# First-layer expert weights in pieces of 512 rows by 512 columns, and wide experts that sum four blocks side by side

## The chip, the cores and the metric

The kernel runs on one core of one Trainium2 chip. The metric is the device time of one execution in microseconds (us). The engines are named as in the profile: PE (TensorE, matmuls), PEld (its weight loads), DVE (VectorE), ACT (ScalarE), POOL (GpSimd) and SP (SyncE, which here only issues DMAs).

## The reference, cut to what matters

One layer of a model with 1024 tokens of width 1024: layer norm, a mixer (attention and a recurrence), layer norm, and then a mixture of 32 experts, of which each token uses 4. The change is in the experts alone.

```python
def clamped_swiglu(hh):
    x_glu = jnp.minimum(hh[..., ::2], SWIGLU_LIMIT)
    x_lin = jnp.clip(hh[..., 1::2], -SWIGLU_LIMIT, SWIGLU_LIMIT)
    return x_glu * jax.nn.sigmoid(SWIGLU_ALPHA * x_glu) * (x_lin + 1.0)
...
    def expert_block(args):
        idx, e = args
        u = clamped_swiglu(h_pad[idx] @ w1[e] + b1[e])
        return u @ w2[e] + b2[e]
```

For one expert `w1` has 1024 rows (the model width) and 2048 columns (a gate column and a linear column for each of 1024 hidden units), and `w2` has 1024 rows and 1024 columns. All of it is float32.

## The kernel before

The mixer and the routing take about the first 1000 us. The routing ranks the experts by their number of tokens, and the kernel gives each rank a fixed capacity: the eleven fullest ranks have room for 136 to 192 tokens (wide experts), the other 21 for 128 (thin experts). A loop for what overflows makes no pass with these inputs. The method `moe` goes through the 32 experts in a fixed order: the first and third are thin, the second and fourth wide, and from then on two thin experts alternate with one wide one, with one thin expert at the end.

Each expert reads 12 pieces of weights of 1 MB, 8 of `w1` and 4 of `w2`, through the method `piece`. A piece arrives by one DMA in a buffer `w` (5 of them). To keep float32 accuracy the kernel multiplies in two parts: ACT makes a rounded copy `wsh` (line 205, two halves of 128 x 1024), and DVE subtracts it to give the rest, `wsl` (line 206, also two halves). There are 4 buffers for such a pair, so at most 4 pieces are split ahead of the matmuls. A `w` buffer is free again when DVE is done with it; a `wsh`/`wsl` buffer is free when the last matmul on that piece is done.

A thin expert (method `first`) keeps its tokens as the stationary operand and streams the weights. Each of four accumulators `acc` (one PSUM bank, 128 x 512) takes two pieces of 256 columns by all 1024 rows: for each piece 8 row blocks, three matmuls each (tokens high by weights high, high by low, low by high; lines 193, 194, 195). ACT and DVE then compute the activation, PE transposes it, and ACT and DVE split the transposes (`uTh`, `uTl`) for the second layer, which streams 512 columns at a time.

A wide expert (method `first_wide`) turns the operands round: 128 weight columns are stationary, and the tokens are streamed, high and low parts side by side (line 1511, up to 384 columns) against `wsh`, and the high part again (line 1513) against `wsl`. Before the change a piece gives two accumulators one after the other (gate and linear part of one block of 128 hidden units), each of 16 matmuls over all 1024 rows. ACT reads an accumulator (line 1515), then DVE (line 1516); only then is its buffer free. There are four accumulator buffers, used in turn by both layers of all experts.

The kernel is written without fixed places in time: the framework's scheduler sets, when the program is built, in which order the instructions stand on each engine, and each engine then works strictly through its list. A DMA is issued on SP's queue when its `w` buffer is free.

Of the kernel before, what the change touches and what calls it, by code (L numbers as in the profile page):

```python
# [10 lines left out]
F32 = mybir.dt.float32  # L11
# [8 lines left out]
P = 128  # L20
# [3 lines left out]
KD = D // P  # L24
# [3 lines left out]
NE = 32  # L28
# [46 lines left out]
def _cols(v):  # L75
    return np.asarray(v).reshape(-1, P).T
# [25 lines left out]
def prep(a):  # L102

    f = lambda n: np.asarray(a[n])
    o = {}
    inv = (np.float32(10000.0) ** (-np.arange(0, 32, 2, dtype=np.float32) / np.float32(32))).astype(np.float32)
    invf = np.tile(np.repeat(inv, 2), 4).reshape(P, 1)
    sgn = np.tile(np.array([-1.0, 1.0], np.float32), 64).reshape(P, 1)
    o["vec"] = np.concatenate(
        [_cols(f("c")), _cols(f("emb_ln_g")), _cols(f("emb_ln_b")), _cols(f("ada_b")[0, :2048]),  # L110
         _cols(f("q_norm_g")), _cols(f("kv_norm_g")), _cols(f("mla_out_g")), _cols(f("rwkv_mu")),
         _cols(f("rwkv_k_k")), _cols(f("rwkv_k_a")), _cols(f("rwkv_r_k")), _cols(f("rwkv_gn_g")),
         _cols(f("rwkv_gn_b")), _cols(f("rwkv_a0")), _cols(f("ln1_g")), _cols(f("ln1_b")), invf, sgn], axis=1)
    o["cst"] = consts()
    o["thr"] = (np.array(CAP)[None, :] + P * np.arange(NB)[:, None]).astype(np.float32)[None]
    o["x"] = f("x")[0]
    o["pos"] = f("positions")
    aw = f("ada_w")[0]
    o["ada1"] = aw[:, :2048].reshape(KD, P, 4, 512).transpose(2, 1, 0, 3)
    o["ada2"] = aw[:, 2048:].reshape(KD, P, 8, 512).transpose(2, 1, 0, 3)  # L120
    o["adab2"] = f("ada_b")[:, 2048:]
    o["rows"] = np.stack([f(n).reshape(-1) for n in ROWS])
    w = f("w_in")[0]
    swap = np.arange(32) ^ 1
    blocks = [w[:, 0:128], w[:, 128:256], w[:, 256:384],
              np.concatenate([w[:, 384:416], w[:, 384:416][:, swap], np.zeros((D, 64), w.dtype)], axis=1)]
    blocks += [w[:, 416 + 128 * i:416 + 128 * (i + 1)] for i in range(14)]
    o["w_in"] = np.stack([b.reshape(KD, P, P).transpose(1, 0, 2) for b in blocks])
    q = f("w_uq")[0].reshape(256, NH, 96)
    rope = q[:, :, 64:].reshape(256, 256)  # L130
    rsw = q[:, :, 64:][:, :, swap].reshape(256, 256)
    q = np.concatenate([q[:, :, :64].reshape(256, 512), rope, rsw], axis=1)
    o["w_uq"] = q.reshape(2, P, 1024).transpose(1, 0, 2)
    o["w_uk"] = f("w_uk")[0]
    o["w_uv"] = f("w_uv")[0]
    o["w2a"] = np.concatenate([f("rwkv_w2")[0], f("rwkv_w0")], axis=0)
    o["a2"] = f("rwkv_a2")[0]
    o["g2"] = f("rwkv_g2")[0]
    o["w_o"] = f("w_o")[0].reshape(KD, P, D).transpose(1, 0, 2)
    o["rw"] = f("router_w")[0].reshape(KD, P, NE).transpose(1, 0, 2)  # L140
    o["rb"] = f("router_b")

    w1 = f("exp_w1")[0].reshape(NE, KD, P, 8, P, 2)
    o["w1"] = w1.transpose(0, 3, 2, 1, 5, 4).reshape(NE, 8, P, KD, 256)
    o["w2"] = f("exp_w2")[0].reshape(NE, 4, 2, P, D).transpose(0, 1, 3, 2, 4)
    b1 = f("exp_b1")[0].reshape(NE, 8, P, 2).transpose(0, 1, 3, 2)

    o["b1r"] = np.concatenate([b1.reshape(NE, 4, 512)] * 2, axis=1)
    o["b2"] = f("exp_b2")[0]
    o["b1c"] = b1.reshape(NE, 16, P).transpose(0, 2, 1)  # L150
    return {k: np.ascontiguousarray(v) for k, v in o.items()}
# [12 lines left out]
class Build:  # L164
# [705 lines left out]
    def head(self, h, oT):  # L870
# [64 lines left out]
        yield  # L935

    def mixers(self, st, left, first, oT, dst):


# [508 lines left out]
    def first(self, e, xT):  # L1448

        nc, mp, pm = self.nc, self.mo, self.pm  # L1450
        V, S, G = nc.vector, nc.scalar, nc.gpsimd
        w1 = self.i["w1"]
        bs = self.biases(e)
        u = mp.tile([P, D], F32, name="u")
        uT = self.split_tile(mp, [P, KD, P], "uT")
        for q in range(4):
            acc = pm.tile([P, 512], F32, name="acc", bufs=4)
            nc.tensor.matmul(acc, self.pick[:, q:q + 1].to_broadcast([P, P]), bs, start=True, stop=False)
            for j in range(2):
                ws = self.piece(w1[bass.ds(e, 1), 2 * q + j].rearrange("o p k n -> (o p) (k n)"))  # L1460
                for k in range(KD):
                    w, c = ws[k // 4], k % 4 * 256
                    self.mm(acc[:, j * 256:(j + 1) * 256], xT[:, k], w[:, c:c + 256],
                            start=False, stop=(j == 1 and k == KD - 1))
            a = acc.rearrange("p (j g f) -> p j g f", j=2, g=2)
            v2 = lambda t: t.rearrange("p (j f) -> p j f", j=2)
            sg = mp.tile([P, 256], F32, name="sg")
            S.activation(v2(sg), a[:, :, 0], AF.Sigmoid, scale=1.702)  # L1468
            ln = mp.tile([P, 256], F32, name="ln")
            V.tensor_scalar(v2(ln), a[:, :, 1], 8.0, -6.0, ALU.min, ALU.max)  # L1470
            V.scalar_tensor_tensor(v2(ln), a[:, :, 0], 7.0, v2(ln), ALU.min, ALU.mult)
            V.scalar_tensor_tensor(u[:, q * 256:(q + 1) * 256], sg, SIG7, ln, ALU.min, ALU.mult)
            if q:
                self.flip(uT, u, 2 * q - 2, 2 * q)
        return [uT], lambda: self.flip(uT, u, 6, 8)
# [14 lines left out]
    def first_wide(self, e, xw, slots):  # L1490

        nc, mp, pm = self.nc, self.mo, self.pm
        V, S, G = nc.vector, nc.scalar, nc.gpsimd
        cap = xw.shape[3]
# [5 lines left out]
        u1 = self.u1  # L1500
        n1 = cap - P
        w1 = self.i["w1"]
        for j in range(KD):
            ws = self.piece(w1[bass.ds(e, 1), j].rearrange("o p k n -> (o p) (k n)"))
            parts = []
            for g in range(2):
                acc = pm.tile([P, 512], F32, name="acc", bufs=4)
                for k in range(KD):
                    w = ws[k // 4]
                    c = slice(k % 4 * 256 + g * P, k % 4 * 256 + (g + 1) * P)  # L1510
                    nc.tensor.matmul(acc[:, 0:2 * cap], w.hi[:, c], xw[:, k].rearrange("p a t -> p (a t)"),  # L1511
                                     start=(k == 0), stop=False)
                    nc.tensor.matmul(acc[:, 0:cap], w.lo[:, c], xw[:, k, 0], start=False, stop=(k == KD - 1))  # L1513
                t = mp.tile([P, cap], F32, name=f"t{g}")
                S.activation(t, acc[:, cap:2 * cap], AF.Identity, bias=bc[:, 2 * j + g:2 * j + g + 1])
                V.tensor_tensor(t, acc[:, 0:cap], t, ALU.add)  # L1516
                parts.append(t)
# [270 lines left out]
```

## Time and profile before

| | |
|---|---|
| median of 3 runs | 2482.98 us (2480.03 to 2487.98) |
| the profiled execution | 2487.42 us |
| its span, first to last instruction | 2485.6 us |
| mean granted PE clock over the span | 0.953 of full speed |
| expert loop, about 995 to 2420 us | PE busy 1385.55 of 1425.00 us, DVE 1286.28 |

The profiled execution is 4.4 us above the median of the runs shown, and 1.8 us of its time lie outside the span. Busy time of PE is a modelled union of overlapping matmuls, so the pace of matmuls is better read from their start times than from their durations.

### The profile page before, as it was taken

How to read it: one execution, taken by the hardware profiler on the slowest of the kernel's cores; microseconds unless marked ns; L12 is line 12 of the kernel's file. 1: busy time of each engine (PE TensorE's matmuls, PEld its weight loads, DVE VectorE, ACT ScalarE, POOL GpSimd, SP SyncE). 2: the span in 40 equal slices, each digit the busy share in tenths (PEclk: the TensorE clock that was granted, in tenths of full speed). 3: DMA queues.
4: the chain of work that ended last, by engine and by line, in shares of the span. 5: the costliest groups of instructions: out<-in, count | busy, mean ns of one | idle time of the engine just before them, and what ended most of it. 6: DMA issues, size and time to landing. Idle time of an engine off the chain costs nothing. (4 is left out here: it accounts for less than half of the span.)

```text
span 2485.6 us, 41948 instructions
## 1 busy us (share of the span) xinstructions
PE 2314.4 (93%) x15523; PEld 1957.1 (79%) x15523; DVE 1994.8 (80%) x3854; ACT 1411.2 (57%) x2357; POOL 558.7 (22%) x411
## 2 busy tenths in 40 slices
PE   6999999999999897799999999999999999999992
PEld 3776766776766685699899898999989988889981
DVE  7666446677766676789898989898979999898987
ACT  5323334444545433566676666676757766666664
POOL 1005222222222444022121212121402121121113
PEclk9999988999989987799999999999999999999996
DMA  6377542212112223779797979797978989797973
GB/s 266 118 258 275 188 112 55 53 45 59 36 40 58 97 96 117 297 279 332 290 339 277 350 275 358 269 359 270 363 265 319 331 307 322 288 334 284 341 279 139
DMA packets 167334, 567.80 MB, mean 228 GB/s; under 512 B 64616, under 2 KB 79737, under 8 KB 116820
## 3 DMA queue, kind: packets, MB, share of 16 engines
q1 hardware_dynamic: 155476, 524.63, 57.4%
q0 software_dynamic: 11216, 39.34, 6.4%
q8 instruction: 124, 2.03, 0.3%
q10 hardware_dynamic: 432, 1.09, 0.1%
q14 instruction: 86, 0.70, 0.1%
HBM read 508.22 MB, written 56.79 MB: 227 GB/s over the span
## 5 line engine op out<-in xcount | busy, mean ns | idle before, releaser
L206 DVE TENSOR_TENSOR wsl<-w,wsh 128x1024 fp32r<-128x1024 f32 x786 | 935.3, 1221 | 139.3 <-ACT wsh L205 138.0
L205 ACT CAST wsh<-w 128x1024 fp32r<-128x1024 f32 x786 | 782.9, 1047 | 348.9 <-PE acc L195 91.0
L193 PE MATMUL acc<-wsh,xTh 128*128 128x256 f32 x1344 | 381.9, 285 | 9.5 <-ACT xTh L205 5.1
L1511 PE MATMUL acc<-xw,wsh 128*128 128x368 f32 (+7 forms) x1408 | 379.0, 352 | 6.4 <-DVE t L1516 6.3
L194 PE MATMUL acc<-wsl,xTh 128*128 128x256 f32 x1344 | 382.8, 285 | 0.7 <-DVE wsl L206 0.7
L195 PE MATMUL acc<-wsh,xTl 128*128 128x256 f32 x1344 | 381.6, 285 | 0.1
L1513 PE MATMUL acc<-xw,wsl 128*128 128x184 f32 (+7 forms) x1408 | 337.2, 240 | 0.0
L1511 PEld LDWEIGHTS acc<-xw,wsh 128*128 128x128 f32 x1408 | 268.0, 190 | 8.5 <-issue 5.2
L1513 PEld LDWEIGHTS acc<-xw,wsl 128*128 128x128 f32 x1408 | 272.2, 193 | 1.0 <-DVE wsl L206 0.2
L193 PEld LDWEIGHTS acc<-wsh,xTh 128*128 128x128 f32 x1344 | 258.5, 193 | 12.6 <-ACT xTh L205 7.0
L194 PEld LDWEIGHTS acc<-wsl,xTh 128*128 128x128 f32 x1344 | 259.5, 193 | 4.8 <-DVE wsl L206 1.0
L195 PEld LDWEIGHTS acc<-wsh,xTl 128*128 128x128 f32 x1344 | 259.2, 193 | 1.5 <-DVE xTl L206 0.3
L1445 POOL DMA_INDIRECT y_d<-y,idx x42 | 147.4, 3509 | 417.9 <-DVE y L1437 327.6
L1348 POOL DMA_INDIRECT xg<-h_d,idx x43 | 92.1, 2142 | 612.9 <-issue 285.0
L193 PE MATMUL acc<-wsh,uTh 128*128 128x512 f32 x512 | 204.5, 402 | 20.3 <-ACT uTh L205 20.3
L194 PE MATMUL acc<-wsl,uTh 128*128 128x512 f32 x512 | 203.2, 397 | 0.0
L195 PE MATMUL acc<-wsh,uTl 128*128 128x512 f32 x512 | 193.5, 405 | 1.8 <-DVE uTl L206 1.8
L193 PEld LDWEIGHTS acc<-wsh,uTh 128*128 128x128 f32 x512 | 97.6, 191 | 42.0 <-ACT uTh L205 23.1
L193 PE MATMUL sm<-hTh,wsh 128*128 128x512 f32 x288 | 116.6, 405 | 7.5 <-ACT wsh L205 2.0
L194 PE MATMUL sm<-hTl,wsh 128*128 128x512 f32 x288 | 117.0, 406 | 4.2 <-DVE hTl L347 3.1
L195 PE MATMUL sm<-hTh,wsl 128*128 128x512 f32 x288 | 115.1, 400 | 0.0
L194 PEld LDWEIGHTS acc<-wsl,uTh 128*128 128x128 f32 x512 | 98.0, 191 | 19.2
(582 smaller groups left out, 4382.0 us busy)
## 6 DMA issues: line engine op xcount, KB each, us to landing
w<-in_w_dram SPq DMA_DIRECT2D x384, 1024.0 KB
aw<-in_ada_dram SPq DMA_DIRECT2D x34, 512.0 KB
w<-in_w_in_dram SPq DMA_DIRECT2D x18, 512.0 KB
aw<-in_ada_dram SPq DMA_DIRECT2D x7, 1024.0 KB
rkv_d<-stage SPq DMA_DIRECT2D x12, 512.0 KB
xt<-in_x_dram SPq DMA_DIRECT2D x8, 512.0 KB
xr<-in_x_dram SPq DMA_DIRECT2D x8, 512.0 KB
xr_d<-xr SPq DMA_DIRECT2D x8, 512.0 KB
```

The lines of the kernel that those rows point to most:

```text
L193: mm(out, a.hi, b.hi, start=start, stop=False)
L194: mm(out, a.hi, b.lo, start=False, stop=False)
L195: mm(out, a.lo, b.hi, start=False, stop=stop)
L205: (hi_eng or self.nc.scalar.copy)(dst.hi, src)
L206: (lo_eng or self.nc.vector).tensor_tensor(dst.lo, src, dst.hi.bitcast(F32), ALU.subtract)
L1348: self.nc.gpsimd.indirect_dma_start(out=xg[0:n], out_offset=None, in_=self.h2_d, in_offset=bass.IndirectOffsetOnAxis(ap=idx[0:n, 0:1], axi ...
L1445: nc.gpsimd.indirect_dma_start(out=self.y_d, out_offset=bass.IndirectOffsetOnAxis(ap=idx[0:n, 0:1], axis=0), in_=y[0:n], in_offset=None, c ...
L1511: nc.tensor.matmul(acc[:, 0:2 * cap], w.hi[:, c], xw[:, k].rearrange("p a t -> p (a t)"), start=(k == 0), stop=False)
L1513: nc.tensor.matmul(acc[:, 0:cap], w.lo[:, c], xw[:, k, 0], start=False, stop=(k == KD - 1))
```

## The change

Pieces of `w1` have another shape: 512 rows by 512 columns in place of 1024 rows by 256 columns. Their size (1 MB, 8 KB for each partition) and number stay, as do the splitting and all of the second layer. In a thin expert an accumulator still takes two pieces, now one for each half of the rows, and each matmul streams 512 columns in place of 256. In a wide expert two pieces hold four blocks of 128 columns; the kernel takes four accumulators at once, runs all four over the first piece, then over the second, and evaluates them as two pairs. Number and shapes of a wide expert's matmuls stay.

```diff
-    w1 = f("exp_w1")[0].reshape(NE, KD, P, 8, P, 2)
-    o["w1"] = w1.transpose(0, 3, 2, 1, 5, 4).reshape(NE, 8, P, KD, 256)
+    w1 = f("exp_w1")[0].reshape(NE, 2, 4, P, 4, 2, P, 2)
+    o["w1"] = w1.transpose(0, 4, 1, 3, 2, 5, 7, 6).reshape(NE, 8, P, 4, 512)
...
-            for j in range(2):
-                ws = self.piece(w1[bass.ds(e, 1), 2 * q + j].rearrange("o p k n -> (o p) (k n)"))
-                for k in range(KD):
-                    w, c = ws[k // 4], k % 4 * 256
-                    self.mm(acc[:, j * 256:(j + 1) * 256], xT[:, k], w[:, c:c + 256],
-                            start=False, stop=(j == 1 and k == KD - 1))
+            for m in range(2):
+                ws = self.piece(w1[bass.ds(e, 1), 2 * q + m].rearrange("o p k n -> (o p) (k n)"))
+                for k in range(4):
+                    c = k % 2 * 512
+                    self.mm(acc, xT[:, 4 * m + k], ws[k // 2][:, c:c + 512], start=False, stop=(m == 1 and k == 3))
...
+        accs = []
         for j in range(KD):
-            ws = self.piece(w1[bass.ds(e, 1), j].rearrange("o p k n -> (o p) (k n)"))
+            if j % 2 == 0:
+
+                accs = [pm.tile([P, 512], F32, name="acc", bufs=4) for _ in range(4)]
+                for m in range(2):
+                    ws = self.piece(w1[bass.ds(e, 1), j + m].rearrange("o p k n -> (o p) (k n)"))
+                    for a, acc in enumerate(accs):
+                        for k in range(4):
+                            w, c = ws[k // 2], slice(k % 2 * 512 + a * P, k % 2 * 512 + (a + 1) * P)
+                            x = xw[:, 4 * m + k]
+                            nc.tensor.matmul(acc[:, 0:2 * cap], w.hi[:, c], x.rearrange("p a t -> p (a t)"),
+                                             start=(m == 0 and k == 0), stop=False)
+                            nc.tensor.matmul(acc[:, 0:cap], w.lo[:, c], x[:, 0], start=False, stop=(m == 1 and k == 3))
             parts = []
             for g in range(2):
-                acc = pm.tile([P, 512], F32, name="acc", bufs=4)
-                for k in range(KD):
-                    w = ws[k // 4]
-                    c = slice(k % 4 * 256 + g * P, k % 4 * 256 + (g + 1) * P)
-                    nc.tensor.matmul(acc[:, 0:2 * cap], w.hi[:, c], xw[:, k].rearrange("p a t -> p (a t)"),
-                                     start=(k == 0), stop=False)
-                    nc.tensor.matmul(acc[:, 0:cap], w.lo[:, c], xw[:, k, 0], start=False, stop=(k == KD - 1))
+                acc = accs[j % 2 * 2 + g]
```

Three places show how the order of instructions changes. In the built program names carry numbers: `acc_13871` is one use of an accumulator buffer, `wsh_13875` one piece; the lines of the wide matmuls move from 1511 and 1513 to 1513 and 1515, and DVE's first read of an accumulator from 1516 to 1521.

On PE, in a thin expert, before: the last two of eight row blocks on one piece, and the first on the next.

```order
L193 MATMUL acc_13871<-wsh_13875,xTh_13719 128x256
L194 MATMUL acc_13871<-wsl_13876,xTh_13719 128x256
L195 MATMUL acc_13871<-wsh_13875,xTl_13720 128x256
L193 MATMUL acc_13871<-wsh_13907,xTh_13719 128x256
L194 MATMUL acc_13871<-wsl_13908,xTh_13719 128x256
L195 MATMUL acc_13871<-wsh_13907,xTl_13720 128x256
```

The same place now: the last of four row blocks on one piece, and the first on the next.

```order
L193 MATMUL acc_13295<-wsh_13299,xTh_13143 128x512
L194 MATMUL acc_13295<-wsl_13300,xTh_13143 128x512
L195 MATMUL acc_13295<-wsh_13299,xTl_13144 128x512
L193 MATMUL acc_13295<-wsh_13319,xTh_13143 128x512
L194 MATMUL acc_13295<-wsl_13320,xTh_13143 128x512
L195 MATMUL acc_13295<-wsh_13319,xTl_13144 128x512
```

A piece had 24 matmuls of 256 columns and has 12 of 512; pieces follow each other in the same way.

On PE, in the fourth wide expert (176 tokens), before: where one accumulator follows another; each has its 16 matmuls in a row, of which the first or last pair stands here.

```order
L1511 MATMUL acc_14443<-xw_14174,wsh_14437 128x352
L1513 MATMUL acc_14443<-xw_14174,wsl_14438 128x176
...
L1511 MATMUL acc_14463<-xw_14174,wsh_14437 128x352
L1513 MATMUL acc_14463<-xw_14174,wsl_14438 128x176
```

The same expert now, from the last matmul of its second group of four to the first of its fourth: 8 matmuls for each accumulator and piece, of which the first stands here.

```order
L1515 MATMUL acc_13766<-xw_13502,wsl_13810 128x176
L1513 MATMUL acc_13877<-xw_13502,wsh_13883 128x352
...
L1513 MATMUL acc_13878<-xw_13502,wsh_13883 128x352
...
L1513 MATMUL acc_13879<-xw_13502,wsh_13883 128x352
...
L1513 MATMUL acc_13877<-xw_13502,wsh_13923 128x352
...
L1513 MATMUL acc_13880<-xw_13502,wsh_13883 128x352
...
L1513 MATMUL acc_13880<-xw_13502,wsh_13923 128x352
...
L1513 MATMUL acc_13991<-xw_13502,wsh_13997 128x352
```

Three accumulators now run over both pieces, and the fourth, `acc_13880`, comes last; it uses the buffer of `acc_13766`, and both pieces stay in use until it is done.

On DVE, in the same expert, before: one piece is split (two halves), then an accumulator is read.

```order
L206 TENSOR_TENSOR wsl_14609<-w_14606,wsh_14608 128x1024 x2
L1516 TENSOR_TENSOR t1_14423<-acc_14406,t1_14423 128x176
L206 TENSOR_TENSOR uTl_14320<-t1_14366,uTh_14319 128x128
L206 TENSOR_TENSOR u1_8922<-t1_14366,u1_8922 128x48
L1516 TENSOR_TENSOR t0_14460<-acc_14443,t0_14460 128x176
```

The same engine now: two pieces are split one after the other, then `acc_13766` is read.

```order
L1521 TENSOR_TENSOR t0_13862<-acc_13765,t0_13862 128x176
L206 TENSOR_TENSOR xTl_14106<-tr_14114,xTh_14105 128x512
L206 TENSOR_TENSOR uTl_13648<-t1_13751,uTh_13647 128x128
L206 TENSOR_TENSOR u1_8922<-t1_13751,u1_8922 128x48
L206 TENSOR_TENSOR wsl_13998<-w_13995,wsh_13997 128x1024 x2
L206 TENSOR_TENSOR wsl_14038<-w_14035,wsh_14037 128x1024 x2
L1521 TENSOR_TENSOR t1_13865<-acc_13766,t1_13865 128x176
L1521 TENSOR_TENSOR t0_13961<-acc_13877,t0_13961 128x176
```

The read that frees the fourth accumulator's buffer now stands behind four halves of weights where it stood behind two.

## Rows read from the trace of the kernel before

**Rows 1.** The page, parts 1 and 2: busy time by engine; granted clock in 40 slices.
```profile
span 2485.6 us, 41948 instructions
PE 2314.4 (93%) x15523; PEld 1957.1 (79%) x15523; DVE 1994.8 (80%) x3854; ACT 1411.2 (57%) x2357; POOL 558.7 (22%) x411
...
PEclk9999988999989987799999999999999999999996
```

**Rows 2.** Busy time by stretch, the whole expert loop.
```profile
core 0: us, PE busy (x) PEld busy (x) DVE busy (x) ACT busy (x) POOL busy (x), PEclk, DMA share, GB/s
995.00:2420.00 1425.00, 1385.55 (x9617) 1273.54 (x9615) 1286.28 (x2070) 961.28 (x1475) 268.99 (x99) 0.98 0.85 310
```

**Rows 3.** The same view: a wide stretch, then a stretch of two thin experts.
```profile
1417.00:1475.00 58.00, 58.00 (x378) 53.25 (x378) 49.53 (x98) 36.87 (x70) 6.49 (x4) 1.00 0.76 270
1475.00:1549.00 74.00, 72.91 (x538) 67.38 (x538) 73.29 (x98) 53.69 (x70) 20.36 (x5) 1.00 0.95 350
```

**Rows 4.** The page, part 5: matmul groups, count, busy, mean ns, idle before.
```profile
L193 PE MATMUL acc<-wsh,xTh 128*128 128x256 f32 x1344 | 381.9, 285 | 9.5 <-ACT xTh L205 5.1
...
L1511 PE MATMUL acc<-xw,wsh 128*128 128x368 f32 (+7 forms) x1408 | 379.0, 352 | 6.4 <-DVE t L1516 6.3
...
L1513 PE MATMUL acc<-xw,wsl 128*128 128x184 f32 (+7 forms) x1408 | 337.2, 240 | 0.0
```

**Rows 5.** PE in order of time, thin experts: start, duration; brackets: idle before.
```profile
1533.21 0.28 PE L193 MATMUL acc<-wsh,xTh 128*128 128x256 f32 x1
...
1536.81 0.28 PE L193 MATMUL acc<-wsh,xTh 128*128 128x256 f32 x1
...
1538.56 0.39 PE L193 MATMUL acc<-wsh,uTh 128*128 128x512 f32 x1
...
1539.92 0.38 PE L1360 MATMUL tr<-csts,u 128*128 128x128 f32 x2
1540.77 0.50 PE L193 MATMUL acc<-wsh,uTh 128*128 128x512 f32 x1 [0.46 <-ACT uTh L205]
```

**Rows 6.** PE in order of time, second layer of the thin expert before.
```profile
1505.79 0.40 PE L193 MATMUL acc<-wsh,uTh 128*128 128x512 f32 x1
...
1507.40 0.39 PE L194 MATMUL acc<-wsl,uTh 128*128 128x512 f32 x1
```

**Rows 7.** Who waited for whom, 1060 to 2400 us: total, times, longest.
```profile
ACT wsh L205 <- PE acc L195: 89.3, 95, 3.3
...
PE acc L193 <- ACT uTh L205: 12.2, 10, 2.6
...
PE acc L1511 <- DVE t L1516: 6.3, 6, 2.0
```

**Rows 8.** PE in a wide expert: last matmul of one accumulator, and of the next.
```profile
1430.98 0.24 PE L1513 MATMUL acc<-xw,wsl 128*128 128x176 f32 x1
...
1433.17 0.24 PE L1513 MATMUL acc<-xw,wsl 128*128 128x176 f32 x1
```

**Rows 9.** ACT in the same stretch.
```profile
1433.37 2.00 ACT L205 CAST wsh<-w 128x1024 fp32r<-128x1024 f32 x2 [1.16 <-PE acc L1511]
1435.27 0.40 ACT L1515 ACTIVATE t<-acc,bc 128x176 f32<-128x176 f32 x1
```

**Rows 10.** DVE in the same stretch.
```profile
1434.45 2.36 DVE L206 TENSOR_TENSOR wsl<-w,wsh 128x1024 fp32r<-128x1024 f32 x2 [0.23 <-ACT wsh L205]
1436.72 0.34 DVE L1516 TENSOR_TENSOR t<-acc,t 128x176 f32<-128x176 f32 x1
```

**Rows 11.** PE at one wait for an accumulator.
```profile
1840.04 0.59 PE L1511 MATMUL acc<-xw,wsh 128*128 128x304 f32 x1 [2.01 <-DVE t L1516]
```

**Rows 12.** Busy time and granted clock around that wait.
```profile
1836.00:1848.00 12.00, 9.99 (x56) 9.85 (x55) 8.87 (x25) 7.75 (x18) 0.00 (x0) 0.72 0.68 250
```

**Rows 13.** PE in the first expert, waiting for its fourth piece.
```profile
1025.66 0.58 PE L193 MATMUL acc<-wsh,xTh 128*128 128x256 f32 x1 [4.38 <-ACT wsh L205]
```

## Prediction, made before the changed kernel ran

> **What bounds the kernel now.** I first read the page for where the time lies. PE is busy 93% of the span and its granted clock is at nine tenths or more in all but the last of the later slices [rows 1], which are the expert loop, where the change is. Then I read busy time by stretch. Over the loop PE is busy 1385.55 of 1425.00 us, DVE 1286.28 [rows 2], so PE sets the pace on average, with about 40 us idle. Next I took one wide and one two-thin stretch apart, since an average over both hides their limits. In the wide stretch PE is busy all 58.00 us and DVE only 49.53; in the thin one PE is busy 72.91 of 74.00 us and DVE 73.29 [rows 3]. So thin experts are limited by two engines at once, and DVE has room only in wide ones. Waits say the same from the other side: ACT waited 89.3 us for PE to free a split-weight buffer in thin first layers, while PE itself waited 12.2 us for `uTh` and 6.3 us for a wide accumulator [rows 7]. The splitters run ahead; PE seldom waits for them. Last I read the pace of matmuls from start times.
>
> **Thin first layers: fewer, longer matmuls.** The 256-column matmuls start every 0.120 us: 30 of them from 1533.21 to 1536.81 [rows 5]. The 512-column matmuls of the second layer have the same float32 type and the same stationary tile size, and start every 0.227 us: 6 from 1538.56 to 1539.92 [rows 5]. A longer look one expert earlier gives 7 in 1.61 us, or 0.230 [rows 6]. Two short ones cost 0.240 us, so one long one saves 0.010 to 0.013 us. Line 193 has 1344 short matmuls [rows 4], lines 194 and 195 as many: 4032 become 2016 of double length. That gives 2016 x 0.010 = 20 us to 2016 x 0.013 = 26 us; I take the middle, 24 us, or 1.15 us for each of 21 thin experts. The weight loads halve with the matmuls and lie beside them, so they are not counted again.
>
> The same rows can be set against a rule. The Trainium skill (TensorE: Matmul & The Clock Gate, section Back-to-back issue gap) gives a warm gap of the columns divided by 2.4 GHz plus about 2.5 ns, that is 109 ns and 216 ns here. By that rule an exchanged pair saves 2.6 ns and all 2016 together some 5 us, an estimate from that page. The trace does not agree with it: its 120 and 227 ns carry 13 to 14 ns of extra for each matmul.
>
> **What stays.** DMAs, ACT casts and DVE splits keep their number and size, and the three streaming matmuls of a row block keep their order; a thin accumulator is complete after the same two pieces. I cost these at nothing: the piece DMAs are hidden by five buffers, and without that cover each late piece would be a wait like the one in the first expert. There PE waited 4.38 us for its fourth piece [rows 13], since the loop has only just begun to load. A faster first layer only waits longer there, so that expert's 1.15 us are not gained: +1 us.
>
> **Wide first layers: the same matmuls, another order.** The 2 x 1408 matmuls of lines 1511 and 1513 [rows 4] keep their shapes, so their own price is zero. What moves is when buffers come free. A pair of matmuls takes 0.274 us (8 pairs from 1430.98 to 1433.17) [rows 8]. Before, a buffer is wanted again after three more accumulators, 3 x 2.19 = 6.6 us. Its readers are done sooner: after the last matmul at 1433.17 ACT first casts a piece (2.00 us), reads at 1435.27 [rows 9], DVE splits that piece (2.36 us) and reads at 1436.72 to 1437.06 [rows 10], 3.9 us in all, so 2.7 us are left over.
>
> After the change I follow `acc_13766`, at the end of a group of four, with the same durations. PE goes on with three accumulators on both pieces: 24 pairs, 6.6 us, and a few transposes or slot matmuls; then `acc_13880` wants its buffer. ACT has two pieces to cast first, and the first of them goes into a buffer that came free 8 matmuls (1.1 us) before the end. So the casts end about 1.1 us less than 2 x 2.00, at +3.0 us, and at +4.1 if ACT is busy when that buffer comes free. DVE can finish the second piece 1.2 us behind the last cast and then read: 4.5 to 5.6 us, and one more us if the small operations listed ahead of the splits are late. The buffer is free 0 to 2 us before it is wanted. Three such hand-overs in each of 11 wide experts make 33. Most fit, some will miss by a few tenths: I take 0.15 us each, +5 us. The bounds are -6 us (the 6.3 us of today's waits vanish [rows 7]) and one more split piece, 2.36 us less 1 us of slack, at each of the 33: +45 us.
>
> **Thin stretches: what DVE gives back.** Two thin experts shrink by 2.3 us on PE, but DVE has 73.29 us of work in a stretch of 74.00 [rows 3], so only 0.7 us are free there. The other 1.6 us must come from the lead: up to four pieces are split ahead, and in the wide stretch DVE idles 8.5 us and can win it back. If the lead covers all, nothing is lost; if it covers none, 1.6 us in each of 9 two-thin stretches, 14 us. What is late next is the chain at the end of a thin first layer, where PE stands between transpose and `uTh` (0.46 us at 1540.77) [rows 5]. I take half, +7 us.
>
> **Sum.** -24 + 1 + 5 + 7 = -11 us. Against its own execution, 2487.42 us, that is 2476 us; that execution lies 4.4 us above the median, so I set it against 2482.98 and predict 2472 us.
>
> **The rivals.**
> *The gain comes whole.* The DVE lead covers the thin stretches and the wide waits go: -24 - 6 = -30, 2453 us. For it speaks ACT's 89.3 us of waiting for PE [rows 7], against it DVE's 99% in thin stretches.
> *DVE becomes the bound in thin experts.* Only 0.7 us of each 2.3 is gained: -24 + 1 + 5 + 14 = -4, 2479 us. For it speaks 73.29 of 74.00 [rows 3].
> *The long matmul takes as long as two short ones.* The 0.227 us were read in the second layer, with other operands; if a first-layer matmul of 512 columns starts only every 0.240 us, the saving is nil, no lead is drawn on, and the wide hand-overs remain: 2483 + 5 = 2488 us, no change. Against it speak both places with long matmuls [rows 5, 6]. The skill's page named above would leave 5 us of saving, so 2483 us.
> *Wide experts stall at the fourth accumulator (the other side).* Both pieces of a group are held until its end, and DVE reads the fourth accumulator only after four halves. It decides from 0.5 us for each of the 33 hand-overs, when it eats what the other terms leave (24 - 1 - 7 = 16 us). At 1.4 us each it costs 45 us: -24 + 1 + 7 + 45 = +29, 2512 us. It can cost more than the wait: after PE had stood 2.01 us for such an accumulator [rows 11] the granted clock of those 12 us was 0.72 [rows 12], so more than half of them ran at 1.2 GHz, which took another 3.4 us.
>
> **How the numbers follow.** A difference of 0.3%, 7.4 us, is about what a measurement of this kernel can tell from none. Chances: the forecast (gain of 5 to 18 us) 0.40, its own range 2465 to 2478 us; the whole gain 0.15; DVE as the bound 0.15; the matmul saving not there 0.10; the wide stall 0.20. Faster takes three quarters of the first (0.30), all of the whole gain and a third of the DVE case (0.05): 0.50. Slower takes the stall and a little of the fourth (0.03): 0.23. The rest is no change: 0.10 + 0.10 + 0.07 = 0.27. The range from 2453 to 2502 us reaches into the whole gain on one side and through half of the stall's on the other.
>
> **What would show it.** Right: thin matmuls of 512 columns starting every 0.227 to 0.230 us, two thin experts in 72 us or a little more with DVE near 100%, wide stretches as long as now. Wrong on the pace: starts further apart than 0.235 us. Wrong on DVE: PE waits for `wsl` or `uTh` grow beyond 20 us in total. Wrong on the wide experts: PE waits on DVE's line 1521 (6.3 us on its line before) above 16 us, and slices with a granted clock under 1.

## The result, and the profile after

The changed kernel takes 2499.46 us (median of 5 runs, 2492.65 to 2500.74) against 2482.98 for the kernel before, ratio of the means 1.0054 with a 95% interval of 1.0029 to 1.0079: slower, by some 13 us (the medians lie 16.5 us apart). Busy time by engine and granted clock on the page, as [rows 1]:

```profile
span 2492.0 us, 37947 instructions
...
PE 2295.2 (92%) x13507; PEld 1846.9 (74%) x13507; DVE 1992.9 (80%) x3854; ACT 1409.0 (57%) x2355; POOL 482.5 (19%) x411
...
PEclk9999999999999987899999999999999999999996
```

PE is busy 19 us less than before, and the span is longer all the same. Busy time by stretch, as [rows 2, 3]: the loop, a wide stretch, three two-thin stretches, a later wide one between them.

```profile
core 0: us, PE busy (x) PEld busy (x) DVE busy (x) ACT busy (x) POOL busy (x), PEclk, DMA share, GB/s
995.00:2420.00 1425.00, 1360.65 (x7558) 1158.21 (x7558) 1278.65 (x2056) 956.84 (x1470) 188.42 (x97) 0.98 0.84 307
1420.00:1478.00 58.00, 58.00 (x370) 53.11 (x369) 49.38 (x98) 37.50 (x70) 6.24 (x4) 1.00 0.73 254
1478.00:1552.00 74.00, 70.64 (x339) 56.58 (x338) 72.74 (x98) 53.07 (x69) 8.45 (x6) 1.00 0.97 362
1609.00:1688.00 79.00, 74.14 (x347) 58.79 (x346) 73.75 (x98) 53.45 (x71) 11.01 (x6) 0.96 0.91 339
2088.00:2143.00 55.00, 54.97 (x377) 49.70 (x377) 46.82 (x99) 36.59 (x70) 5.67 (x4) 1.00 0.75 266
2143.00:2221.00 78.00, 72.22 (x344) 58.08 (x343) 73.51 (x98) 53.02 (x69) 13.27 (x6) 0.98 0.90 342
```

Wide stretches are full of PE work, as before. In 74 us of two thin experts PE is busy 70.64 us where it was busy 72.91 [rows 3], but from 1609 us on they take 78 us and more, with PE idle for 5 to 6 of them. Who waited for whom on PE, 1060 to 2400 us, as [rows 7]:

```profile
PE acc L193 <- ACT uTh L205: 18.3, 16, 1.9
PE acc L195 <- DVE uTl L206: 12.5, 10, 1.7
PE tr L1316 <- DVE uTl L206: 10.6, 9, 1.2
...
PE acc L1513 <- DVE t L1521: 3.5, 1, 3.5
```

The waits of the first three lines, which all end with a split transpose (`uTh`, `uTl`), are 41.4 us; the same three were 12.9 us before (12.2 of them [rows 7]). The third is that of the small one-hot matmuls (`td`, line 1316), which need a PSUM buffer that `uTl` frees. The wide experts' waits went from 6.3 us in six to 3.5 us in one (line 1521 is 1516 of before), which lies in the first wide expert:

```profile
1079.47 0.66 PE L1513 MATMUL acc<-xw,wsh 128*128 128x384 f32 x1 [3.54 <-DVE t L1521]
```

Most of the new waits lie where the first of two thin experts goes over to its second layer. One such place on PE in order of time:

```profile
1626.81 0.39 PE L193 MATMUL acc<-wsh,xTh 128*128 128x512 f32 x1
...
1631.34 0.39 PE L195 MATMUL acc<-wsh,xTl 128*128 128x512 f32 x1
1631.57 0.79 PE L1360 MATMUL tr<-csts,u 128*128 128x128 f32 x4
1634.13 0.50 PE L193 MATMUL acc<-wsh,uTh 128*128 128x512 f32 x1 [1.77 <-ACT uTh L205]
...
1637.13 1.22 PE L195 MATMUL acc<-wsh,uTl 128*128 128x512 f32 x2 [0.66 <-DVE uTl L206]
```

Twenty matmuls from 1626.81 to 1631.34 start every 0.227 us: the pace is as forecast. Then four transposes stand in one batch behind the whole first layer, with the second layer right behind them. Before, in every stretch of two thin experts, the transposes of the first two quarters of `u` stood two and two, the first two with 31 to 44 first-layer matmuls behind them.

The batch stands in six of the nine two-thin stretches, those from 1609 us on, and these take 78.2 to 79.1 us. In the first three the transposes still stand two and two, with five first-layer and four second-layer matmuls between them, and these take 74.6 to 74.7 us. The same place in the third of them:

```profile
1499.05 0.38 PE L1360 MATMUL tr<-csts,u 128*128 128x128 f32 x2
...
1501.35 0.38 PE L1360 MATMUL tr<-csts,u 128*128 128x128 f32 x2
1501.82 0.47 PE L1458 MATMUL acc<-bs,pick 128*128 128x512 f32 x1
1503.24 0.73 PE L195 MATMUL acc<-wsh,uTl 128*128 128x512 f32 x2 [0.95 <-DVE uTl L206]
```

ACT and DVE at the place with the batch:

```profile
1631.81 1.99 ACT L205 CAST wsh<-w 128x1024 fp32r<-128x1024 f32 x2 [0.72 <-PE acc L195]
1633.71 0.36 ACT L205 CAST uTh<-tr 128x256 fp32r<-128x256 f32 x1
...
1631.80 3.48 DVE L206 TENSOR_TENSOR wsl<-w,wsh 128x1024 fp32r<-128x1024 f32 x3
1635.20 0.41 DVE L1470 SCALAR_TENSOR_TENSOR ln<-acc,ln 128x256 f32<-128x256 f32 x1
1635.54 1.20 DVE L206 TENSOR_TENSOR wsl<-w,wsh 128x1024 fp32r<-128x1024 f32 x1
1636.67 0.41 DVE L206 TENSOR_TENSOR uTl<-tr,uTh 128x256 fp32r<-128x256 f32 x1
```

`uTh` stands behind two casts, `uTl` behind four halves of weights. Then the clock, over the next 6.8 us:

```profile
1634.90:1641.70 6.80, 6.03 (x14) 3.89 (x13) 3.93 (x9) 0.71 (x1) 0.00 (x0) 0.50 0.98 405
```

0.50 is 1.2 GHz. From 1015 to 2400 us, after has eight stretches at 0.50, 37 us together (before five, 24 us); while PE is busy they cost half their length. Six of the eight, 24 us, lie right behind the six batches.

From the first expert's first weight matmul to the last expert's last, the loop took 1441.6 us before and 1451.5 after: the eleven wide stretches 629.3 and 624.6, the eleven thin ones (two single, nine double) 759.7 and 777.0, the last expert 52.6 and 49.8. The loss lies in thin stretches alone, 16.5 us of it in those six.

### The profile page after: what moved, and what is told of

Its sections match the earlier page's. It is cut to its first block, busy times and chain, and to the rows that moved or that the text cites. A ratio compares the mean times of both kernels' runs of the same rounds, so it can differ in the third digit from the quotient of the medians.

```text
span 2492.0 us, 37947 instructions
## 1 busy us (share of the span) xinstructions
PE 2295.2 (92%) x13507; PEld 1846.9 (74%) x13507; DVE 1992.9 (80%) x3854; ACT 1409.0 (57%) x2355; POOL 482.5 (19%) x411
## 4 chain that ended last, share of the span: by engine, by line
PE 32%; DVE 20%; issue 5%; ACT 2%; DMA 1%; SPq 0%; POOLq 0%; POOL 0%; DVEq 0%; ACTq 0%
DVE wsl L206 14%; PE acc L1513 10%; PE acc L195 5%; PE acc L193 5%; PE acc L194 5%; PE acc L1515 4%; ACT wsh L205 1%; DMA w<-in_w_dram 1%; PE tr L1360 1%; PE acc L1425 1%; DVE ln L1469 1%; PE acc L1421 1%; DVE uTl L206 1%; DVE ln L1470 1%; DVE oh L1312 1%
## 5 line engine op out<-in xcount | busy, mean ns | idle before, releaser
L193 PE MATMUL acc<-wsh,xTh 128*128 128x512 f32 x672 | 263.1, 394 | 4.7 <-ACT wsh L205 4.7
L194 PE MATMUL acc<-wsl,xTh 128*128 128x512 f32 x672 | 264.3, 393 | 0.5 <-DVE wsl L206 0.5
L195 PE MATMUL acc<-wsh,xTl 128*128 128x512 f32 x672 | 263.6, 392 | 0.0
L1445 POOL DMA_INDIRECT y_d<-y,idx x42 | 119.0, 2833 | 502.7 <-DVE y L1437 392.9
L195 PE MATMUL acc<-wsh,uTl 128*128 128x512 f32 x512 | 200.3, 416 | 12.9 <-DVE uTl L206 12.7
L1348 POOL DMA_INDIRECT xg<-h_d,idx x43 | 58.8, 1366 | 610.2 <-DVE xTl L206 219.1
L193 PEld LDWEIGHTS acc<-wsh,xTh 128*128 128x128 f32 x672 | 127.2, 189 | 31.4 <-ACT wsh L205 5.0
L194 PEld LDWEIGHTS acc<-wsl,xTh 128*128 128x128 f32 x672 | 127.2, 189 | 27.7 <-DVE wsl L206 1.0
L195 PEld LDWEIGHTS acc<-wsh,xTl 128*128 128x128 f32 x672 | 127.0, 189 | 26.7 <-DVE xTl L206 0.2
L195 PEld LDWEIGHTS acc<-wsh,uTl 128*128 128x128 f32 x512 | 95.7, 195 | 39.5 <-DVE uTl L206 21.2
```

The source lines that it names most:

```text
L193: mm(out, a.hi, b.hi, start=start, stop=False)
L194: mm(out, a.hi, b.lo, start=False, stop=False)
L195: mm(out, a.lo, b.hi, start=False, stop=stop)
L1348: self.nc.gpsimd.indirect_dma_start(out=xg[0:n], out_offset=None, in_=self.h2_d, in_offset=bass.IndirectOffsetOnAxis(ap=idx[0:n, 0:1], axi ...
L1445: nc.gpsimd.indirect_dma_start(out=self.y_d, out_offset=bass.IndirectOffsetOnAxis(ap=idx[0:n, 0:1], axis=0), in_=y[0:n], in_offset=None, c ...
```

## Experiments

The theories: **order** (the loss is the new place of the transposes and of `uT` in the lists); against it **DVE** (two thin experts are bound by DVE's 73.7 us of work, whatever PE does) and **wide** (the four accumulators side by side cost it). **Queue** and **place**, further down, divide the first: what stands ahead of `uTh` and `uTl`, or the batch itself.

All ran beside the kernel before. The table has for each the ratio to it with its interval, and from one profiled execution the loop, the mean of the nine two-thin stretches (first weight matmul of the first to first of the wide expert behind), and PE's idle time in the loop (its length less PE's busy time). The time ahead of the loop differs by up to 16 us between executions, so loops are the sharper comparison.

| kernel | ratio (95%) | loop | two thin | PE idle |
|---|---|---|---|---|
| before | 1 | 1441.6 | 75.1 | 41.7 |
| after | 1.0054 (1.0029 to 1.0079) | 1451.5 | 77.2 | 66.2 |
| short_matmuls | 0.9973 (0.9950 to 0.9995) | 1439.5 | 76.2 | 42.6 |
| wide_in_turn | 1.0050 (1.0031 to 1.0070) | 1456.2 | 77.7 | 68.2 |
| u_in_time | 0.9995 (0.9971 to 1.0018) | 1422.6 | 69.4 | 41.3 |
| before_u_in_time | 1.0052 (1.0034 to 1.0069) | 1459.5 | 70.8 | 49.2 |
| two_turns_early | 0.9950 (0.9929 to 0.9970) | 1429.4 | 74.9 | 54.5 |
| turns_spread | 0.9982 (0.9963 to 1.0001) | 1440.4 | 75.1 | 62.8 |
| before_batch | 0.9965 (0.9948 to 0.9983) | 1438.1 | 75.9 | 42.9 |
| fourth_piece_later | 0.9976 (0.9959 to 0.9994) | 1439.1 | 75.5 | 58.6 |
| fourth_piece_and_turns | 0.9984 (0.9965 to 1.0003) | 1433.2 | 75.2 | 58.2 |
| next_piece_too | 0.9975 (0.9959 to 0.9991) | 1430.1 | 75.0 | 54.2 |
| before_fourth_later | 1.0120 (1.0093 to 1.0147) | 1469.1 | 77.3 | 54.8 |
| half_on_gpsimd | 1.0023 (1.0004 to 1.0041) | 1444.6 | 77.5 | 63.4 |
| less_dve_turns_early | 0.9864 (0.9842 to 0.9885) | 1405.8 | 73.3 | 34.6 |
| less_dve_before | 0.9888 (0.9866 to 0.9910) | 1407.6 | 73.2 | 21.8 |
| less_dve_after | 0.9905 (0.9885 to 0.9925) | 1422.6 | 74.6 | 47.5 |
| least_dve_turns_early | 0.9741 (0.9717 to 0.9765) | 1377.0 | 70.4 | 14.9 |
| least_dve_before | 0.9909 (0.9886 to 0.9932) | 1412.4 | 72.6 | 23.4 |

**Which part of the change: the thin matmuls, or the wide experts.**

```diff
-  self.mm(acc, xT[:, 4*m+k], ws[k//2][:, c:c+512], start=False, stop=(m == 1 and k == 3))
+  for h in (0, 256):   # short_matmuls
+      self.mm(acc[:, h:h+256], xT[:, 4*m+k], ws[k//2][:, c+h:c+h+256], start=False, ...)
...
-  for m in range(2):   # wide_in_turn: both pieces first, then accumulator by accumulator
-      ws = self.piece(...)
-      for a, acc in enumerate(accs):
+  pcs = [self.piece(...) for m in range(2)]
+  for a, acc in enumerate(accs):
+      for m, ws in enumerate(pcs):
```

> The changed kernel, but each 512-column matmul of the thin first layers is cut in two of 256 columns again; pieces, layout and the four accumulators of a wide expert stay. In its order the transposes of the first of two thin experts stand two and two again, the first two of the batch with 16 first-layer matmuls behind them. Order theory (the loss is that four transposes stand in one batch at the end of the first thin expert, with nothing to cover ACT and DVE): the waits of PE for uTh, uTl there (41 us in the changed kernel) fall below 20 us, time 2476 to 2488 us. Wide theory (the four accumulators side by side cost the time): no change from the changed kernel, 2494 to 2504 us. DVE theory (two thin experts are bound by DVE's 73.7 us of work, the pace of PE is without effect): no change either, 2494 to 2504 us.

> The changed kernel, but a wide expert fills its four accumulators one after the other, 16 matmuls each over both pieces, instead of side by side; both pieces are then held until the fourth. Order theory: the batch of four transposes is still there in the order, so the waits stay: 2494 to 2504 us. Wide theory: the loss goes with the side-by-side sums, 2470 to 2486 us. DVE theory: 2494 to 2504 us.

The loss goes with the long matmuls and stays with the wide experts in turn: wide theory out. New pieces, new layout and four accumulators with short matmuls are as fast as before or a little faster. But that gain lies in wide stretches (618.0 us together, against 629.3 before); two thin experts still take 76.2 us there, so half of what they lost stays. wide_in_turn gives one comparison more: its list has the batch from the third two-thin stretch on, and this one takes 79.5 us, where after, without the batch at that place, takes 74.7.

**The order of u.** `issue_after(x)` lists what its block makes behind `x` on the engine of `x`, without waiting for it.

```diff
+  self.behind[self.pieces + 3] = ui      # ui: last step of a quarter of u, on DVE
...
+  with self.tc.issue_after(self.behind.pop(self.pieces).ins):   # in piece(), where there is one
       for c in CUT:
           self.split(ws[:, slice(*c)], w[:, slice(*c)])
```

> The changed kernel with one thing more: on DVE the split of the third piece after a quarter of u is listed behind the last step of that quarter, so that u no longer stands behind five or more pieces. In its order the transposes then stand two and two, each with 11 to 23 first-layer matmuls behind them. All work is as in the changed kernel. Order theory: PE's waits for uTh, uTl and the slots' one-hot (41 us) fall below 12 us, the half-clock stretches behind them go too (7 stretches, some 13 us), two thin experts take 71 to 74 us instead of 78; time 2455 to 2475 us. DVE theory: DVE's work is the same, so two thin experts still take 76 us or more; 2490 to 2504 us. Wide theory: no change, 2494 to 2504 us.

> The kernel before with the same listing of u on DVE (the split of the third piece after a quarter of u behind that quarter's last step), and nothing of the change. Order theory: the kernel before loses little in that place (12 us of waits for uTh), so it gains little: 2472 to 2484 us; and the changed kernel with the same listing is then 12 to 25 us faster than this one, which is the pace of the long matmuls. DVE theory: 2480 to 2486 us, and the changed kernel with the same listing is no faster than it.

> A second look at the changed kernel with u in time, whose profiled run took 2474 us and whose median is 2487 us. If the difference lies ahead of the expert loop, the loop takes 1423 us again (first to last expert matmul); if it lies in the loop, more half-clock stretches stand in it than the five of the first look.

PE's waits for `uTh` and `uTl` are gone from u_in_time, and it is as fast as before: 0.6% better than after, as order theory says in kind, but 12 us short of it. The second look took 2483 us with a loop of 1433.4 us, so its spread lies in the loop too; it does not lie in the clock, since that loop has four stretches at 1.2 GHz from 1015 us on where the expectation had more than five. What two thin experts gain (their stretch also ends earlier, since the next wide expert's first matmuls now stand among their last) the wide ones lose: 61.8 us on average instead of 56.8, with new waits on `wsl`. The same edge makes the kernel before slower, which neither theory expected. With this edge the long matmuls are some 14 us ahead of the short ones, as order theory says and DVE theory does not; but the short kernel pays for other things too there, 18.2 us of waits for `xw` (a wide expert's tokens) and nine stretches at 1.2 GHz, so this pair does not show the worth of the pace alone.

**Fewer moves.** two_turns_early moves two transposes, turns_spread four; before_batch forces the batch on the kernel before.

```diff
+  with self.tc.issue_after(turned[1].ins):   # two_turns_early: for q == 3, m == 1 alone
       for k in range(4):
           self.mm(acc, xT[:, 4*m+k], ...)
...
+  for t in turns_of_quarters_0_and_1:          # before_batch: behind the last first-layer matmul
+      self.tc.add_manual_dep(t.ins, last.ins.name, NoSync)
```

> The changed kernel with one edge more in its order: the last twelve first-layer matmuls of a thin expert stand behind the transposes of the first quarter of u, so that in the first of two thin experts two of the batch of four transposes are covered by them; the order of the wide experts stays. Order theory: the waits of PE for uTh, uTl and the one-hot (41 us in the changed kernel) fall to 15 to 25 us, the half-clock stretch behind each batch goes, two thin experts take 74 to 76 us instead of 78; time 2480 to 2491 us, ratio to the kernel before 0.996 to 1.001. DVE theory (DVE's 73.7 us of work is the limit, the wait only shows it): the time that is not waited for at the batch is waited for at the next split; no change from the changed kernel, ratio 1.003 to 1.007.

> The changed kernel with two edges: the first piece of the last quarter of a thin first layer stands behind the transposes of the first quarter of u, its second piece behind those of the second. In the order the transposes then stand two, twelve matmuls and six second-layer pairs, two. Order theory: waits for uTh, uTl and the one-hot fall below 15 us; 2472 to 2488 us, ratio 0.994 to 1.000, at least as good as with the one edge. DVE theory: ratio 1.003 to 1.007. A third outcome would be that PE now stands at the transposes themselves, since u is late on DVE: then waits of PE for u appear and the ratio stays above 1.003.

> The kernel before, its short matmuls and its wide experts, with nothing but the batch forced into its order: in the first of two thin experts the transposes of the first two quarters of u stand behind the whole first layer. Order theory: the loss of the changed kernel appears without the change: 9 such places, 2 to 4 us each with the half clock behind it, ratio 1.006 to 1.014, and PE's waits for uTh and uTl above 25 us (12 before). DVE theory: ratio 0.999 to 1.002.

One edge, and the changed kernel goes from 1.0054 to 0.9950. Waits of PE with two_turns_early; then one of its two-thin stretches:

```profile
PE acc L195 <- DVE uTl L206: 13.5, 11, 1.6
PE tr L1316 <- DVE uTl L206: 11.4, 9, 1.4
PE acc L193 <- ACT uTh L205: 7.3, 10, 0.9
```

```profile
1876.10:1951.00 74.90, 70.92 (x348) 57.24 (x347) 73.70 (x99) 53.40 (x71) 12.99 (x6) 1.00 0.97 358
```

turns_spread was slower than two_turns_early: PE now stood 6.5 us at the transposes for `u`, the third outcome in part. With two_turns_early the waits fell by only 9 us, to 32.2, but they got shorter (1.6 us at most), and from 1100 to 2400 us no stretch at 1.2 GHz is left. DVE is busy 73.70 of 74.90 us. All nine two-thin stretches now take 74.6 to 75.0 us, as the three of after without the batch. before_batch speaks against the batch as the whole cause: there the wait for `uTh` grew to

```profile
PE acc L193 <- ACT uTh L205: 22.3, 11, 2.5
```

from 12.2, yet the kernel got faster, which neither theory expected. Its thin stretches did get longer, by 6.6 us together (766.3 against 759.7); its wide ones got 10.8 us shorter (618.5 against 629.3), where the new list waits 0.8 us instead of 6.3.

**What stands ahead of uT.**

```diff
+  for t in self.uT_of_quarter_1: es.enter_context(self.tc.issue_after(t.ins))   # ACT and DVE
   ws += self.piece(w2[..., q])      # q == 3, thin experts
```

> The changed kernel with the batch of transposes left at the end of the first thin layer, but on ACT and DVE the cast and split of the fourth second-layer piece are listed behind the halves of uT of the second quarter, so that those no longer stand behind 2.0 us of cast and 2.4 us of split. Queue theory (what costs is what stands ahead of uTh and uTl on ACT and DVE when PE comes for them): PE's waits before the second layer (39 us) fall below 15 us, the half-clock stretch behind the batch goes, ratio to the kernel before 0.994 to 1.001. Place theory (the batch itself costs, having no matmuls behind it): the 1.8 us wait stays in large part, ratio 1.002 to 1.007. DVE theory: what is not waited there is waited at the postponed piece, ratio 1.003 to 1.007.

> The changed kernel with both edits: twelve first-layer matmuls behind the transposes of the first quarter, and the fourth second-layer piece behind uT of the second. Queue theory: PE's waits before the second layer fall below 10 us (25 with the first edit alone, 39 without), those before the one-hot's matmuls stay near 20 us; ratio 0.990 to 0.995. DVE theory: no better than with the first edit alone, 0.994 to 0.997.

> As the run before, and the second piece of the next expert is listed behind uT of the third quarter on ACT and DVE, which frees the transposes' bank that the one-hot's matmuls wait for (20 us of waits). Queue theory: those waits fall below 8 us as well, all idle time of PE in the loop is below 35 us, ratio 0.986 to 0.992. DVE theory: the waits move to the late pieces, ratio 0.994 to 0.998.

> The kernel before with the listing of the fourth second-layer piece behind uT of the second quarter, and nothing of the change. Queue theory: the 12 us of waits for uTh shrink, ratio 0.995 to 1.000; the changed kernel with the same edit is 12 us or more below it, the worth of its pace. DVE theory: 0.998 to 1.002, and no difference of more than 6 us between the two.

Mending what stands ahead of `uT` takes the loss away too (PE's waits before the second layer 20 us, between the two expectations). It does not leave the batch as it was, though: in seven of the nine two-thin stretches the transposes follow the whole first layer, but the scheduler now lists two, four second-layer matmuls, two. So queue and place are not told apart. The mends don't add up, and queue theory's ratios for the second and third were missed: all of them stop at 75 us for two thin experts, whichever waits are left, as DVE theory says. On the kernel before, the same edge costs 1.2%, which neither theory expected, and the two kernels with it lie 36 us apart where DVE theory allowed 6: before_fourth_later has 13 stretches at 1.2 GHz from 1015 to 2400 us instead of five.

**DVE's work.** Part of it left out, as the expectations say; or half a piece of it moved.

```diff
   for c in CUT:
+      if cut and c[0]:            # second half of the chosen w2 pieces, thin experts
+          nc.scalar.copy(ws.hi[:, 1024:2048], w[:, 1024:2048])
+          return ws[:, 0:1024], Split(ws.hi[:, 1024:2048], ws.hi[:, 1024:2048])
       self.split(ws[:, slice(*c)], w[:, slice(*c)])    # half_on_gpsimd: lo_eng=nc.gpsimd there
```

> The changed kernel with two turns early, in which a part of DVE's work is left out: in thin experts the low part of the second half of the second and fourth second-layer piece isn't computed (the matmuls read the high part in its place), 2.36 us of DVE less for each thin expert, 4.7 us for two; PE's and ACT's work and the order of PE stay. DVE theory (after the order is mended two thin experts take 75.0 us because DVE has 73.7 us of work in them, wherever PE then waits): they fall to 71 to 73 us, where PE's own 70.6 us stop them; the loop is 20 to 32 us shorter than the 1429 us with two turns early, ratio 0.984 to 0.988. Queue theory (single waits at single places are left): 74 to 75 us, ratio 0.993 to 0.996.

> The kernel before with the same part of DVE's work left out. DVE theory: here PE has 72.9 us of its own in two thin experts that take 74 to 77 us, so less is to be had than with long matmuls: 73 to 74.5 us, loop 5 to 18 us shorter, ratio 0.993 to 0.998; the kernel with long matmuls and the same work left out is then 18 to 25 us faster than this one, which is the pace of the long matmuls in full. Queue theory: 0.997 to 1.001.

> The changed kernel, its order of PE kept with the batch of four transposes, with the same part of DVE's work left out; in it one half less also stands ahead of uTl at the batch. DVE theory with the order's cost on top: 78 us fall to 73 to 75.5 us, ratio 0.988 to 0.998. If the batch alone sets the loss: still 77 us or more, ratio above 1.000.

> The changed kernel with two turns early, complete in its work: the low part of the second half of the second second-layer piece of thin experts is computed by GpSimd instead of DVE, 1.18 us of DVE less for each thin expert, 2.4 us for two. DVE theory: two thin experts take 72.7 to 73.5 us instead of 75.0, ratio 0.988 to 0.993, provided that GpSimd's subtraction, which no trace so far shows in this place, isn't late for the matmuls that read it; if it is late, PE waits on that piece and the ratio is 0.995 or more. Queue theory: 0.993 to 0.997.

> As less_dve_turns_early, but the low part of the second half of all four second-layer pieces of thin experts is left out, 4.7 us of DVE less for each thin expert, so DVE has some 64 us of work in two thin experts that took 73.2 us with half as much left out. If DVE was still part of the limit: 71 to 72.2 us for two thin experts, loop 1386 to 1398 us. If the weight stream is now the limit (its DMA share was 0.97 there): 72.8 to 73.5 us and ACT waits on the pieces' DMAs grow beyond 20 us. If it is the chain from transpose over uTh and uTl to the second layer at the end of a first layer: 72.8 to 73.5 us and PE's waits for uTh, uTl stay near 20 us.

> The kernel before with the same left out. PE was busy 72.5 of 73 us in two thin experts with half as much left out, so it is its own limit: 72.5 to 73.5 us whatever DVE does, loop 1400 to 1410 us. If two thin experts fall below 72.5 us here, PE was not the limit. The kernel with long matmuls and the same left out is 8 to 20 us faster than this one if DVE was what kept its pace from paying, and within 5 us of it if the DMA stream or the chain does.

In the less_dve and least_dve kernels a part of the result is not computed. One two-thin stretch of each, busy time as above: less_dve_turns_early, less_dve_before, least_dve_turns_early, least_dve_before.

```profile
1854.00:1927.30 73.30, 70.76 (x349) 57.37 (x347) 70.47 (x96) 53.49 (x71) 12.98 (x6) 1.00 0.97 366
```

```profile
1857.10:1930.40 73.30, 72.84 (x541) 67.57 (x539) 69.82 (x95) 53.51 (x71) 11.73 (x6) 1.00 0.98 360
```

```profile
1841.30:1911.60 70.30, 70.30 (x349) 57.20 (x348) 66.29 (x92) 54.10 (x71) 15.81 (x6) 1.00 0.98 367
```

```profile
1851.10:1923.70 72.60, 72.60 (x540) 67.56 (x539) 66.15 (x91) 53.98 (x71) 13.64 (x5) 1.00 0.96 352
```

With DVE's work in full, long and short matmuls both take 75 us; with some left out, both some 73.2; with twice as much left out, PE is busy all the time in both, and the long ones are 2.3 us faster, which is the whole gain in pace (2 x 1.15). less_dve_after, with the batch in its later stretches, came out between (74.6 us), as expected. The first step missed what I expected of it: long was to be 18 to 25 us ahead there and was 2 us ahead by the loop. The second speaks for DVE: 1377.0 against 1412.4 us, more than the 8 to 20 expected, 22 of the 35 us in thin stretches and the rest in wide ones, where the short kernel now waits 8 us for accumulators. The weight stream is not the limit, since its share stayed at 0.98 while the stretch fell by 3 us. Not separated: the halves left out are also fewer halves ahead of `uTl`, so part of the effect may be that chain rather than DVE's total. And the order did not stay as expected: with less to split, the scheduler lists transposes and second-layer matmuls otherwise, most of all in the least_dve pair.

half_on_gpsimd, with all work done, was slower than two_turns_early, and PE waited 8.3 us for GpSimd's halves. These halves, DVE's in one two-thin stretch (shortest, median and longest, ns), and the longest of DVE with the half of GpSimd beside it:

```profile
L206 POOL TENSOR_TENSOR wsl<-w,wsh 128x1024 fp32r<-128x1024 f32 x19 | 79.4, 4181 | 102.9 <-ACT wsh L205 79.0 <-PE acc L195 23.9
```

```profile
L206 DVE TENSOR_TENSOR wsl<-w,wsh x47: 1202/1212/3130, 1879.1 to 1956.6; 128x1024 fp32r<-128x1024 f32 x47
```

```profile
1940.77 2.39 POOL L206 TENSOR_TENSOR wsl<-w,wsh 128x1024 fp32r<-128x1024 f32 x1 [8.83 <-ACT wsh L205]
...
1941.12 3.13 DVE L206 TENSOR_TENSOR wsl<-w,wsh 128x1024 fp32r<-128x1024 f32 x1
```

## Why the prediction was wrong

I forecast 2472 us, 11 us faster; by the ratio it became some 13 us slower.

- **Thin first layers, -24 us: right** (23 is the middle of the 20 to 26 that it was taken from). Starts every 0.227 us. PE's busy time over the loop fell from 1399.9 to 1385.3 us although stretches at 1.2 GHz cost it 6.8 us more (37.4 less 23.8, halved): some 21 us less work. By the gap that the Trainium skill (TensorE: Matmul & The Clock Gate, Back-to-back issue gap) gives for an isolated matmul it would have been 5 us, an estimate from that page; the 0.227 us lie 11 ns above that gap.
- **Wide hand-overs, +5 us: small, as said, but of the other sign.** The wide stretches got 4.7 us shorter, inside the bounds. Today's waits did vanish, in three later experts that became 10 us shorter together. The rival's stall, DVE's read behind splits of weights, came once in 33 hand-overs, 3.5 us in the first wide expert, with 6.8 us at 1.2 GHz, and that expert took 65.8 us instead of 60.0. wide_in_turn, with the same stall (3.3 us), shows that the sums side by side cost nothing.
- **What stays, at nothing: this step failed.** I followed the weight matmuls in the new order and let the transposes be. The scheduler moved them behind the first layer in six of nine two-thin stretches, and `uT` behind more splits. By two_turns_early against after, thin stretches and last expert together, that costs 20.6 us (756.8 + 49.4 against 777.0 + 49.8), up to 12 of them by the clock behind the batch.
- **Thin stretches, what DVE gives back, +7 us (0 to 14): mis-sized.** In the mended order these stretches are 6.1 us shorter than before (3.2 of them in the last expert) where pace alone, less the first expert's, gives 23: DVE and its hand-overs to PE take back 17, and two thin experts gain only 0.3 of 2.3 us each. Where before had no longer wait, in its first four two-thin stretches, it took 74.0 to 74.1 us with 73.3 us of DVE work [rows 3]; the first three of after, without the batch, took 74.6 to 74.7. Between these the pace gained nothing. I counted on the lead from the wide stretch, where DVE idles 8.5 us. At most four pieces are split ahead, which I take to be why DVE doesn't win that time back; no run had more buffers. The rival of DVE as the bound named the mechanism, and its sign, waits for `uTh` and `uTl` above 20 us, came.

The two errors come to +31 us (20.6 + 17 - 7) and the wide term takes 10 off: instead of 11 us shorter the loop is 10 us longer. That the order costs the one part is shown by two edges that each take it away, and by the stretches with and without the batch in the same execution. That DVE's splits hold the pace back is supported by the pairs of kernels with work left out, not shown by them alone, since their order changes too. Why the same kind of edge hurts the kernel before is not settled beyond its waits and its clock.

two_turns_early is faster than both kernels: by the ratios some 12 us below before and 26 below after (22 by the loops).

## What to carry to other kernels

Look for a second engine that is as busy in the same stretch before counting on a faster matmul: beside a DVE that was 98% busy the long matmuls were worth 0.3 us for two thin experts, and 2.3 us with DVE relieved. When a scheduler writes the order, look after a change of shape at the small operations (transposes, their copies and splits) between two stages, not only at the matmuls that were changed: two transposes moved by twelve matmuls were worth 1% here. And judge a change by more than one order, since the same edge gained 0.8% in one of these kernels and lost 1.2% in the other.

## What the runs showed of the hardware

A subtraction of 128 x 1024 took GpSimd 4181 ns on average (2.39 to 6.45 us) where DVE takes 1.2 us. Of the 49 DVE splits in the loop that overlapped one, 35 took 1.20 to 1.23 us as elsewhere and 14 took 2.40 to 3.13: the stretch had 75.81 us of DVE work instead of 73.70, although a half for each expert had been taken from it.

After the first batch's wait of 1.77 us PE ran 6.8 us at 1.2 GHz, and behind each of the other five batches 3.4; in two_turns_early, waits of up to 1.6 us at the same places were followed by no such stretch. The length of a wait alone does not tell, though: of the nine waits of 2.2 to 2.5 us behind the batch in before_batch, four were followed by 3.4 us at 1.2 GHz and five were not.
